# Fifteen small transfers on ScalarE's queue of a masked prefix-sum kernel

## The chip, the cores and the metric

The kernel runs on one core of a Trainium2 chip. The metric is the device time of one execution in microseconds; the time before is the median of 8 runs. A profile of one execution is read beside it: its span runs from the first instruction to the last.

## The reference

For each of 8 batches, x is masked beyond the batch's length, summed along the sequence, and the running sum at the middle of the length is taken; that row is multiplied by w.

```python
B, S, D = 8, 8192, 512                       # x [B,S,D], w [D,D], float32
mask = (pos < lengths[:, None, None])
cs = np.cumsum(x * mask, axis=1)
mid_features = cs[b_idx, lengths // 2, :]
return np.matmul(mid_features[:, None, :], w).squeeze(1)
```

Only one row of the running sum is used, so what has to be computed for each batch is the sum of the first lengths//2 + 1 rows that are below the length, and then a product of 8 rows with w. With the lengths drawn, most of the time goes to reading some 27 MB of x.

## The kernel before

**Tiling.** x is cut into units of 8 rows (8 x 512 floats, 16 KB). A chunk is 128 units, one for each partition: 2 MB. The first 256 rows of each batch come as two front chunks, by two plain transfers on SP's queue at the start. The units beyond are packed: VectorE computes from the lengths how many chunks there are and a table `idx` of unit numbers, and GpSimd fetches each chunk by an indirect DMA (11 of them here). A last part is fetched in two halves into `xl`, then 256 rows (from row 256 on) of two batches into `xb`, and w in three slices into `wt`.

**Ring.** Chunks land in four slots of `xt`. TensorE multiplies a chunk's units with 0/1 weights (`wr`, made by VectorE, copied into the slot by ScalarE) and adds into `s_ps`, 8 matmul calls a chunk (16 matmul records). When a chunk is done, GpSimd issues the gather that reuses its slot (`gather`, at L243 through `fetch`), and ScalarE copies the weights of the chunk that comes there (`weigh`, L206). SP's `relay` (L174) waits for the weights and for the landing and tells TensorE, which waits at L455. Between chunks TensorE runs idle matmuls (L446) into an unused bank.

**End.** The last part, `xb`, the folding of the partial sums (`mf_ps`), and the product with w (`o_ps`) follow. VectorE copies one half of the output and SP stores it; ScalarE copies the other half (L215) and stores it itself (L222). GpSimd waits for both stores.

**ScalarE's program** is what the change touches, in `scalar`. In its order: the transfer of the lengths (L516, issued ahead of the program's branch), the clearing of `xl` (L187, `s_zero`), a wait for VectorE's mark "w", a load of `count` (L191), the copy of the weights of the last part (L194, `wl`), the weights of chunks 2 and 3 (L198), the ring of `weigh`, the two copies of the output and the store. GpSimd waits for `s_zero` before it fetches into `xl`. Each engine issues its transfers on a queue of its own (SP q1, ScalarE q10, GpSimd q0); all are carried out by the same 16 DMA engines of the core. A transfer raises its semaphore by 16 when all of it has landed.

Of the kernel before, what the change touches and what calls it, by code (L numbers as in the profile page):

```python
# [11 lines left out]
P = 128  # L12
# [3 lines left out]
def kernel(  # L16
# [17 lines left out]
    B, S, D = x.shape  # L34
# [23 lines left out]
    def sb(name, shape, dt=F32):  # L58
        return ctx.enter_context(nc.sbuf_tensor(name, shape, dt))

    def ps(name, shape):
        return ctx.enter_context(nc.psum_tensor(name, shape, F32))

    def sem(name):
        return tc.alloc_semaphore(name)
# [52 lines left out]
    c_sb = sb("c_sb", [P, P])  # L118
    mf_sb = sb("mf_sb", [P, KC, B])
    o_sb = sb("o_sb", [P, D // 2])  # L120

    s_ps = ps("s_ps", [P, D])
    c_ps = ps("c_ps", [P, D])
# [7 lines left out]
    s_front = [sem(f"front{k}") for k in range(FRONT)]  # L131
    s_last = [sem(f"last{k}") for k in range(HALF)]
    s_back = [sem(f"back{k}") for k in range(BB)]
    s_w = [sem(f"w{k}") for k in range(3)]
    s_len, s_out, s_pool, s_dve, s_pe, s_done, s_wr, s_rdy, s_zero, s_act, s_wl, s_now = (
        sem(n) for n in ("len", "out", "pool", "dve", "pe", "done", "wr", "rdy", "zero", "act", "wl", "now"))
# [6 lines left out]
    def weights_of(s):  # L143
        return wr[:, s * U * B:(s + 1) * U * B]

    def ring(eng, name, left, body):
        for s in range(R):
            with nc.body(f"{name}_0_{s}", valid_engines=[eng.engine]):
                eng.br_cmp(left, s, f"{name}_1_{s}", f"{name}_end", "IS_GT")  # L149
            with nc.body(f"{name}_1_{s}", valid_engines=[eng.engine]):  # L150
                body(s)
                if s == R - 1:
                    eng.reg_sub(left, left, R)
                eng.br(f"{name}_0_{(s + 1) % R}")
# [30 lines left out]

    def scalar(act):
        act.memzero(xl[:]).then_inc(s_zero, 1)  # L187
        left = act.alloc_register("left_act")
        free = act.alloc_register("free_act")
        act.wait_ge(s_dve, marks["w"])  # L190
        act.load(left, count[:])  # L191
        act.reg_sub(left, left, 1)
        last = act.snap(left)
        act.copy(out=wl[:], in_=wc[:, bass.ds(last, 1)].rearrange("p c e -> p (c e)"),  # L194
                 ).then_inc(s_wl, 1)
        act.reg_add(left, left, FRONT)
        for s in range(FRONT, R):
            act.copy(out=weights_of(s), in_=wc[:, s - FRONT]).then_inc(s_wr, 1)  # L198
        act.reg_sub(left, left, R)
        act.reg_mov(free, 1)  # L200
        act.br("ac_0_0")

        def weigh(s):
            act.wait_ge(s_done, free)
            col = act.snap(free)
            act.copy(out=weights_of(s),  # L206
                     in_=wc[:, bass.ds(col + (R - FRONT - 1), 1)].rearrange("p c e -> p (c e)"),
                     ).then_inc(s_wr, 1)
            act.reg_add(free, free, 1)

        ring(act, "ac", left, weigh)
        with nc.body("ac_end", valid_engines=[act.engine]):
            act.wait_ge(s_pe, 6)
            for j in range(2):
                act.copy(out=o_sb[64:64 + B, j * P:(j + 1) * P],  # L215
                         in_=o_ps[64 + 32 * j:64 + 32 * j + B, :P]).then_inc(s_act, 1)
            act.wait_ge(s_act, 2)
            store(act, 1)
            act.br(END)

    def store(eng, g):
        eng.dma_start(out=out[:, HALVES[g]], in_=o_sb[64 * g:64 * g + B]).then_inc(s_out, 16)  # L222
# [201 lines left out]
    def tensor(pe):  # L424
# [81 lines left out]
        with nc.body("pe_pad", valid_engines=[pe.engine]):  # L506
            for _ in range(PAD):
                pe.wait_ge(s_dve, 1)
            pe.br("pe_0")

    programs = [(nc.vector, vector, "dv"), (nc.sync, sync, "sy"), (nc.scalar, scalar, "ac"),
                (nc.gpsimd, gpsimd, "gp")]
    for f in range(FRONT):
# [42 lines left out]
```

## Time and profile before

| what | us |
|---|---|
| median of 8 runs | 83.33 |
| lowest and highest of them | 82.88, 84.48 |
| the profiled execution | 82.9 |
| its span | 81.1 |
| TensorE busy, weight loads beside it | 56.6, 15.0 |
| VectorE, ScalarE, GpSimd busy | 14.1, 8.1, 20.5 |

The span has 1120 instructions, and the granted clock is 0.997. The transfers, from the profile's rows of DMA queues:

```profile
DMA packets 2789, 31.25 MB, mean 385 GB/s; under 512 B 370, under 2 KB 386, under 8 KB 898
q1 hardware_dynamic: 304, 4.20, 12.4%
q8 instruction: 1, 0.02, 0.1%
q14 instruction: 2, 0.02, 0.0%
```

Each row gives packets, megabytes and the time that the packets took as a share of 16 engines' span. In the timelines below a row is: start in us, length in us, engine, line, operation, output<-input, number, and in brackets the idle time ahead of it with what ended it. A row of stages gives the stage, its length, the busy time of PE, PEld, DVE, ACT and POOL with the number of instructions, the granted clock, the DMA share and the GB/s.

### The profile page before, as it was taken

To read this page: it belongs to the slowest core of one execution; us is meant where nothing else is said; L and a number is where in the kernel's file an instruction comes from. 1 tells how busy PE (TensorE), PEld (TensorE's weight loads), DVE (VectorE), ACT (ScalarE), POOL (GpSimd) and SP (SyncE) were. 2 spreads that over 40 slices of the span, in tenths; PEclk is the share of its full clock that TensorE was granted. 3 is DMA by queue.
4 is the path that set the end of the run, shared out by engine and by line. 5 is a ranking of instruction groups with operands and counts; after the bars stand their busy time and mean duration, and the time that the engine had idled before them with its cause. 6 is when DMAs were issued, how large, how long until landed. Compare 5 with 4: busy or idle time off the path is not lost. (4 is left out here: it accounts for less than half of the span.)

```text
span 81.1 us, 1120 instructions
## 1 busy us (share of the span) xinstructions
PE 56.6 (70%) x358; PEld 15.0 (19%) x358; DVE 14.1 (17%) x58; ACT 8.1 (10%) x16; POOL 20.5 (25%) x43
## 2 busy tenths in 40 slices
PE   1962399996939589393975939679394984848830
PEld 1462121212102021120201102021120201005600
DVE  4738899610000000000000000000000000004220
ACT  2991000310100001010010100100000000000020
POOL 4400644524050501405032050569600000000000
PEclk9999999999999999999999999999999999999998
DMA  0999999999999999999999999999999999999400
GB/s 0 364 412 388 493 404 396 461 412 408 420 445 428 420 437 433 420 437 429 437 428 428 420 445 420 429 437 428 420 437 437 412 408 412 404 412 408 178 0 8
DMA packets 2789, 31.25 MB, mean 385 GB/s; under 512 B 370, under 2 KB 386, under 8 KB 898
## 3 DMA queue, kind: packets, MB, share of 16 engines
q0 software_dynamic: 2464, 27.00, 78.9%
q1 hardware_dynamic: 304, 4.20, 12.4%
q8 instruction: 1, 0.02, 0.1%
q10 hardware_dynamic: 18, 0.01, 0.0%
q14 instruction: 2, 0.02, 0.0%
HBM read 31.46 MB, written 0.02 MB: 388 GB/s over the span
## 5 line engine op out<-in xcount | busy, mean ns | idle before, releaser
L426 PE MATMUL s_ps<-xt,wr 128*8 128x512 f32 x208 | 26.1, 621 | 15.1 <-PEq L455 15.1
L446 PE MATMUL idle_ps<-rank,v_f 128*4 128x512 f32 x48 | 22.6, 593 | 0.0
L426 PEld LDWEIGHTS s_ps<-xt,wr 128*8 128x8 f32 x208 | 5.0, 90 | 34.9 <-issue 34.9
L243 POOL DMA_INDIRECT xt<-in_x_dram,now x9 | 9.2, 1021 | 8.0 <-POOLq L269 8.0
L298 DVE COPY s_sb<-s_ps 128x256 f32<-128x256 f32 x2 | 0.8, 424 | 56.9 <-PE s_ps L426 56.8
L267 POOL COPY now<-idx 128x1 int32 x9 | 2.5, 279 | 22.1 <-PE s_ps L426 22.1
L446 PEld LDWEIGHTS idle_ps<-rank,v_f 128*4 128x4 f32 x48 | 4.2, 88 | 16.6 <-issue 16.6
L206 ACT COPY wr<-wc 128x64 f32 x9 | 2.2, 244 | 32.9 <-PE s_ps L426 32.7
L243 POOL DMA_INDIRECT xt<-in_x_dram,idx x2 | 2.2, 1119 | 5.8 <-DVE at_f L298 5.5
L187 ACT ACTIVATE xl<-xl 128x4096 uint32<-128x4096 uint32 x1 | 3.6, 3617 | 0.0
L434 PE MATMUL s_ps<-zero 1*128 1x512 f32 x2 | 2.1, 1136 | 1.8 <-DVE jump L298 1.8
L215 ACT COPY o_sb<-o_ps 8x128 f32<-8x128 f32 x2 | 0.5, 256 | 26.9 <-PE o_ps L426 26.9
L426 PE MATMUL s_ps<-xl,wl 128*8 128x512 f32 x16 | 2.1, 594 | 1.3 <-DMA xl<-in_x_dram,idx_h 1.3
L298 DVE TENSOR_TENSOR wc<-early,ge 128x1984 f32<-128x1984 f32 x1 | 2.2, 2225 | 0.0
L298 DVE TENSOR_TENSOR early<-v,b_ps 128x1984 f32<-128x1984 f32 x1 | 2.2, 2222 | 0.0
L438 PE MATMUL b_ps<-row,ones 1*128 1x16 f32 x2 | 0.6, 380 | 2.3 <-DVE row L298 2.3
L243 POOL DMA_INDIRECT xl<-in_x_dram,idx_h x2 | 2.0, 992 | 0.6 <-issue 0.6
L426 PE MATMUL c_ps<-xb,wb 128*2 128x128 f32 x32 | 1.3, 276 | 0.3 <-DMA xb<-in_x_dram 0.2
L187 ACT ACT_TABLE_LOAD x1 | 1.3, 1283 | 1.5 <-SPq L56 1.5
L426 PE MATMUL o_ps<-wt,mf_sb 128*8 128x128 f32 x32 | 1.2, 273 | 0.3 <-DVE mf_sb L298 0.3
L492 PE MATMUL mf_ps<-fold,s_sb 128*128 128x8 f32 x8 | 1.2, 264 | 0.0
L492 PEld LDWEIGHTS mf_ps<-fold,s_sb 128*128 128x128 f32 x8 | 1.1, 193 | 0.5 <-issue 0.5
(74 smaller groups left out, 22.9 us busy)
## 6 DMA issues: line engine op xcount, KB each, us to landing
xt<-in_x_dram SPq DMA_DIRECT2D x2, 2048.0 KB, 10.4
xb<-in_x_dram POOLq DMA_DIRECT2D x2, 512.0 KB, 18.4
wt<-in_w_dram POOLq DMA_DIRECT2D x1, 512.0 KB, 19.5
wt<-in_w_dram POOLq DMA_DIRECT2D x2, 256.0 KB, 19.6
xt<-in_x_dram,now POOLq DMA_INDIRECT x9, 16.0
xt<-in_x_dram,idx POOLq DMA_INDIRECT x2, 11.9
xl<-in_x_dram,idx_h POOLq DMA_INDIRECT x2, 17.3
lens<-in_lengths_dram ACTq DMA_DIRECT2D x1, 0.1 KB
```

The source lines that it names most:

```text
L187: act.memzero(xl[:]).then_inc(s_zero, 1)
L206: act.copy(out=weights_of(s), in_=wc[:, bass.ds(col + (R - FRONT - 1), 1)].rearrange("p c e -> p (c e)"),).then_inc(s_wr, 1)
L215: act.copy(out=o_sb[64:64 + B, j * P:(j + 1) * P], in_=o_ps[64 + 32 * j:64 + 32 * j + B, :P]).then_inc(s_act, 1)
L243: pool.indirect_dma_start(out=to, out_offset=None, in_=units, in_offset=bass.IndirectOffsetOnAxis(ap=at, axis=0), bounds_check=n - 1, oob_ ...
L267: pool.tensor_copy(out=now[:, s:s + 1], in_=idx[:, bass.ds(col + (R - FRONT - 1), 1)],).then_inc(s_now, 1)
L298: do(*args, **kw).then_inc(s_dve, 1)
L426: return pe.matmul(to[32 * j:32 * j + weights.shape[1], :rows.shape[1]], lhsT=weights, rhs=rows, start=False, stop=False, skip_group_check ...
L434: pe.matmul(to[:, :width], lhsT=zero[:, :P], rhs=zero[:, :width], start=True, stop=False, skip_group_check=True)
L438: pe.matmul(to[:, :of.shape[1]], lhsT=ones[:], rhs=of[:], start=True, stop=True,).then_inc(s_pe, 1)
L446: pe.matmul(idle_ps[:FB], lhsT=v_f[:, 0], rhs=rank[:].to_broadcast((P, D)), start=True, stop=True, skip_group_check=True)
L492: pe.matmul(mf_ps[:, B * k:B * (k + 1)], lhsT=s_sb[:, at], rhs=fold[:], start=False, stop=False, skip_group_check=True)
```

## The change

A tile `small` of 128 x 512 floats and a semaphore `s_small` are added. Behind the clearing of `xl` ScalarE issues fifteen transfers: the k-th takes the first k rows and k+16 columns of w into k rows of `small`, at a column of its own. Nothing reads `small`. Ahead of its store ScalarE waits until `s_small` has reached 240, that is, until all fifteen have landed. No other instruction is added, removed or moved on any engine.

```diff
     o_sb = sb("o_sb", [P, D // 2])
+    small = sb("small", [P, D])
...
     s_back = [sem(f"back{k}") for k in range(BB)]
+    s_small = sem("small")
...
     def scalar(act):
         act.memzero(xl[:]).then_inc(s_zero, 1)
+        for k in range(1, 16):
+            act.dma_start(out=small[:k, 32 * k:33 * k + 16], in_=w[:k, :k + 16]).then_inc(s_small, 16)
         left = act.alloc_register("left_act")
...
             act.wait_ge(s_act, 2)
+            act.wait_ge(s_small, 240)
             store(act, 1)
```

## The prediction

> **What bounds the kernel now.** I read the page's strip of slices first, then the stages by windows, then the chain that ended last, then ScalarE's own timeline, and at last the single packets and the landing records of the DMA rows.
>
> ```profile
> DMA  0999999999999999999999999999999999999400
> q0 software_dynamic: 2464, 27.00, 78.9%
> q10 hardware_dynamic: 18, 0.01, 0.0%
> L426 PE MATMUL s_ps<-xt,wr 128*8 128x512 f32 x208 | 26.1, 621 | 15.1 <-PEq L455 15.1
> ```
>
> The 16 DMA engines are 90% busy or more in 36 slices of 40; TensorE idles 15.1 us ahead of its chunk matmuls, at L455, where it waits for a chunk to land. ScalarE's queue is q10: 18 packets, nearly nothing.
>
> ```profile
> 13.00:19.00 6.00, 5.14 (x28) 0.99 (x30) 2.74 (x10) 1.02 (x5) 3.18 (x4) 1.00 1.03 434
> 19.00:35.00 16.00, 12.10 (x76) 2.52 (x76) 0.00 (x0) 0.73 (x3) 3.71 (x7) 1.00 1.00 427
> 35.00:55.00 20.00, 14.81 (x89) 2.97 (x82) 0.00 (x0) 0.98 (x4) 6.38 (x10) 1.00 1.01 430
> ```
>
> The last two numbers of each stage are the DMA share and GB/s: full, at 427 to 434. One chunk is 2 MB, 8 packets of 16 KB on each engine; the packets' rows say 611 ns each, and 8 x 0.611 = 4.89 us is the period of the chunks. So the end is set by DMA time, and by the DMA engine that finishes last.
>
> ```profile
> 55.98 18.73 DMA xb<-in_x_dram
> 74.71 0.04 issue
> 74.75 0.63 PE c_ps L426 x12
> ```
> ```profile
> 77.30 0.12 PEld L426 LDWEIGHTS o_ps<-wt,mf_sb 128*8 128x8 f32 x8 [0.24 <-DMA wt<-in_w_dram]
> ```
>
> The chain ends in the landing of xb, and its last matmuls wait for the last slice of w, which landed at 77.26. That landing is a record of 16 marks, one for each engine: twelve between 76.18 and 76.47, then 76.64, 76.90, 77.16 and 77.26. Four engines lag, and two of them (call them A and C) are 0.7 to 1.0 us behind the twelve. Each lag starts at a code packet: 16 KB on q8 at 2.22 (927 ns), and 8 KB on q14 at 19.34 and 30.88 (314 and 309 ns), after which the next data packet took 1107, 1136 and 881 ns. From then on the lags stay the same to the end. Twelve engines have 0.79 to 1.08 us to spare, the others 0.62, 0.36, 0.10 and 0: what is added on an engine with time to spare costs nothing, what is added on A or C moves the end one for one.
>
> ```profile
> 0.92 0.53 ACTq L516 DMA_DIRECT2D lens<-in_lengths_dram  x1
> 1.49 1.28 ACT L187 ACT_TABLE_LOAD   x1 [1.49 <-SPq L56]
> 2.79 3.62 ACT L187 ACTIVATE xl<-xl 128x4096 uint32<-128x4096 uint32 x1
> 15.29 0.25 ACT L194 COPY wl<-wc 128x64 f32 x1 [8.88 <-DVE wb L298]
> 78.34 0.56 ACTq L222 DMA_DIRECT2D out_dram<-o_sb  x1
> ```
>
> **Part 1: fifteen issues on ScalarE's sequencer.** A row costs 0.53 (lens, one packet) or 0.56 us (the store, eight); SP's two of 128 packets took 1.30 together. So 15 x 0.53 to 15 x 0.66 = 8.0 to 9.9 us. They stand behind the clearing of xl and before the wait for VectorE's w mark. In this trace ScalarE's register steps run before its copies are done (the step of L199 at 15.43, the second copy of L198 at 15.58), so I let the issues start near 2.8, beside the clearing, and end near 11 to 13; at the latest they start when it ends, at 6.41, and end at 14.4 to 16.3. The w mark lets ScalarE go at 14.38 before. At worst its copies come 1.9 us later. What is queued behind them is wl (used at 70.05) and the weights of chunk 2: the first of these is copied at 15.44, and that chunk lands at 18.79, so over 3 us cover it. Past that, TensorE would take chunk 2 late, and GpSimd's next gather would wait; but gathers land 16 us after their issue at one each 4.9 us, so some 11 us of transfers are queued. Cost 0; it costs something only if ScalarE is late by more than these 11 us. Nothing else is passed: lens is issued ahead of the fifteen, SP's front transfers and GpSimd's gathers are on other queues.
>
> A page speaks against such transfers: the Trainium skill, "DMA: Bandwidth & Descriptors", sections "Anatomy of one DMA — SWDGE (gpsimd) path" and "Rules for kernel authors", gives each a fixed 2.0 us, mostly overhead below 64 KB, so by it fifteen in a row would be an estimated 30 us. The row nearest is lens, 0.92 to its landing at 2.11, 1.19 us; fifteen of that in a row would be 18 us. Neither is on a path here, because nothing waits for one transfer before the next is issued, and the wait for all of them stands at 78 us.
>
> **Part 2: packets on the DMA engines.** Transfer k has k rows of (k+16) x 4 bytes, 68 to 124: 120 packets, 12.6 KB, in bytes 0.03 us of the 427 GB/s. What counts is the time per packet on one engine. The lens transfer of one row left one mark beside one packet, the store of 8 rows eight marks: each row goes to an engine of its own. So an engine gets at most 15 of the small packets and the mean over the engines is 7.5; which engine gets how many is not in the trace.
>
> The cost of one, from both sides. Low end: lens's packet of 64 bytes took 8 ns and a semaphore packet 9, and a gap of 4 ns stands between packets: 8 + 9 + 2 x 4 = 25 ns. A change of queue: at 12.4 to 12.7 the engines pass from q1 to q0, and the first 16 KB packet of q0 took 611 to 616 ns on ten of them and up to 820 on the others, 651 in the mean, 40 ns over; so 65 ns with that. High end: the store's 1 KB packets took 46 to 99 ns, and the packet after a code fetch lost 0.27 to 0.52 us. I take 25 to 65, since those small packets and that change of queue are of the same kind, with 45 in the middle. On A and C: 7.5 packets each in the mean, and the larger of two shares is near 10, so 10 x 0.045 = 0.45 us; the ends are 0 (A and C get none) and 15 x 0.065 = 0.98. The packets themselves can give no gain: the twelve engines at 611 ns run at their own pace and give nothing back to A and C.
>
> The same page, section "Why a DMA increments its semaphore by 16 and not by 1", says that k rows use the lowest-numbered k engines, which gives engine 0 fifteen and engine 14 one. It leaves open which numbers A and C have, so it changes the spread and not the mean.
>
> **Part 3: the last wait.** s_small reached 240 long before; the wait itself is one more instruction on ScalarE ahead of its store, 17 to 46 ns by other semaphore rows. The packets of SP's store start last (79.38 against 79.34), which covers it: 0 to 0.04, I take 0. The tile and the semaphore cost nothing.
>
> **The sum.** 0 + 0.45 + 0 on the profiled execution: span 81.1 to 81.5, time 82.9 to 83.35. That execution is 0.43 us below the median of 83.33 over 8 runs (82.88 to 84.48), so by the median 83.33 + 0.4 = 83.7.
>
> **The rivals.**
> 1. Hidden altogether: A and C get few small packets, or a packet costs its 17 ns alone. For it: twelve engines have 0.8 us or more to spare. Against it: C and A both have to be missed. Time 83.3.
> 2. Slower, each small packet breaks the stream of its engine. For it: the 0.27 to 0.52 us lost behind each code packet, which is also a lone packet of another queue. Against it: the change from q1 to q0 lost nothing on ten engines. At 0.1 us (the 1 KB rows) an engine with 15 of them is 1.5 us late, less up to 1.0 to spare: +0.5 to +1.5, about 84.4. At 0.27 it is 4.05 less 0.8: about 86.6. It decides from 0.09 us a packet on, where ten of them on A pass 1%.
> 3. One more code fetch: fifteen instructions more may push ScalarE's code over a block. One 8 KB packet with its loss is 0.31 + 0.27 to 0.31 + 0.52 on one engine, 0.6 to 0.8, which counts in full on A or C only: with part 2, up to 84.6.
> 4. Faster: the moved code lets a fetch fall on another engine. Without A and C's lag the end could come 0.4 us earlier, with all four gone 0.8, so that even this hardly reaches 1%: 82.5.
>
> **How the numbers follow.** My forecast (0.1 to 0.9 us, 83.4 to 84.2) 0.60; hidden 0.14; rival 2 0.17; rival 3 0.06; rival 4 0.03. A measurement here can tell about 1%, 0.8 us. Slower by more: rivals 2 and 3, and a little of my own upper end, 0.25; faster 0.03; within 1% 0.72. Range: from 83.0, just under the hidden case, to 84.9, which takes in the 0.1 us of rival 2 and rival 3, and leaves the broken stream out. The likeliest time is 83.7.
>
> **What would show it.** q10 should hold 258 packets (18 + 120 rows + 120 marks). ScalarE's queue should show fifteen issues of 0.53 to 0.66 us; a start before 6.4 shows that they pass the clearing, and wl should still come near 15.3. The chunk period should stay 4.89, and the waits of SP at L174 as they were. The 16 marks of the last landing decide part 2: if the last comes 0.1 to 0.9 us later and the middle of the twelve by less than that, the packets cost what I say. Packets of 16 KB of 700 ns and more beside the small ones, between 3 and 13 us, would show rival 2; a further packet on q8 or q14 rival 3. I am wrong if the stages from 19 to 55 us change their rate, since nothing of the change is left by then.

## The result, and the profile after

The changed kernel took 83.96 us in the median of 22 runs (83.55 to 84.93), the kernel before 83.28 us beside it (59 runs). The ratio is 1.0077, with a 95% interval of 1.0056 to 1.0099: 0.5 to 0.8 us slower, within the 1% that the forecast had as its likeliest case. Measured twice more, on two chips, the same change gave 1.0033 [1.0003, 1.0063] and 1.0029 [1.0005, 1.0054], some 0.25 us. The ratios leave out the single runs that a lower granted clock made slow, so they are not the quotients of the medians. Its profiled execution took 83.85 us, its span 82.0 us against 81.1.

First ScalarE's timeline of the changed kernel (start, length, engine, line, what):

```profile
0.92 0.53 ACTq L521 DMA_DIRECT2D lens<-in_lengths_dram  x1
1.48 1.28 ACT L189 ACT_TABLE_LOAD   x1 [1.48 <-SPq L56]
1.55 1.37 ACTq L191 DMA_DIRECT2D small<-in_w_dram  x4
2.78 3.62 ACT L189 ACTIVATE xl<-xl 128x4096 uint32<-128x4096 uint32 x1
2.94 4.25 ACTq L191 DMA_DIRECT2D small<-in_w_dram  x11
15.29 0.24 ACT L198 COPY wl<-wc 128x64 f32 x1 [8.89 <-DVE wb L303]
```

The fifteen issues begin before the clearing of `xl` has begun and run beside it; they take 5.6 us, 0.37 us each, and end at 7.2. The copy of `wl` stands at 15.29 as before. Then the page's rows of queues:

```profile
q10 hardware_dynamic: 258, 0.02, 0.2%
q8 instruction: 1, 0.02, 0.1%
q14 instruction: 2, 0.02, 0.0%
```

258 packets on ScalarE's queue, the 18 of before and 240 new ones (120 rows, 120 semaphore marks), and no further code packet. The chain still ends in the landing of `xb`, which comes 0.93 us later (75.64 against 74.71) at the same 18.73 us from issue to landing, and its last matmuls still wait for w:

```profile
56.92 18.73 DMA xb<-in_x_dram
75.64 0.04 issue
75.69 0.64 PE c_ps L431 x14
```
```profile
78.21 0.12 PEld L431 LDWEIGHTS o_ps<-wt,mf_sb 128*8 128x8 f32 x8 [0.21 <-DMA wt<-in_w_dram]
```

So the loss is made before 56 us and carried to the end. SP's waits for the landings say that it is made at the first gathers: for the two gathers with `idx` it waits 0.9 us longer, for the nine behind them as long as before (total, times, longest). Before, then with the change:

```profile
SPq L174 <- DMA xt<-in_x_dram,now: 42.0, 9, 4.7
SPq L174 <- DMA xt<-in_x_dram,idx: 8.9, 2, 4.7
```
```profile
SPq L176 <- DMA xt<-in_x_dram,now: 42.0, 9, 4.7
SPq L176 <- DMA xt<-in_x_dram,idx: 9.8, 2, 5.6
```

The stages show the place. A row gives the stage, its length, busy time of PE, PEld, DVE, ACT and POOL, the granted clock, the DMA share and the GB/s. Before:

```profile
9.00:12.40 3.40, 2.86 (x16) 0.61 (x17) 3.26 (x6) 0.00 (x0) 1.78 (x2) 1.00 0.96 410
12.40:13.60 1.20, 1.20 (x7) 0.26 (x3) 1.20 (x1) 0.00 (x0) 0.28 (x1) 1.00 0.96 396
13.60:18.00 4.40, 4.23 (x23) 0.73 (x20) 2.14 (x10) 1.02 (x5) 1.99 (x3) 1.00 1.02 428
```

With the change:

```profile
9.00:12.40 3.40, 2.86 (x16) 0.60 (x17) 3.26 (x6) 0.00 (x0) 1.78 (x2) 1.00 0.99 406
12.40:13.60 1.20, 1.20 (x5) 0.13 (x1) 1.20 (x1) 0.00 (x0) 0.00 (x0) 1.00 0.81 318
13.60:18.00 4.40, 4.40 (x22) 0.97 (x21) 2.14 (x10) 0.78 (x4) 1.74 (x2) 1.00 1.04 440
```

The middle rows differ. At 12.4 to 13.6 us the engines pass from the front transfers (q1) to the gathers (q0), which is called the hand-over below; there the DMA share is 0.81 where it was 0.96, and the rate 318 GB/s where it was 396. From 19 us on the stages run at 425 to 434 GB/s, as before.

The landing records say who is late. Each line holds marks of the last slice of w, one an engine, in us:

```
before   first 76.19, middle 76.38, last five 76.47 76.64 76.90 77.16 77.26
change   first 76.69, middle 76.83, last five 77.21 77.24 77.34 77.51 78.17
```

The middle moved by 0.45 us and the last by 0.91. The last engine is the one that took the 8 KB code packet at 19.07 us (309 ns, and 1146 for the data packet behind it): the last mark of the gather ahead of it stood 0.52 us behind the middle, that of the next 1.43. Before, one engine jumped the same way (code packet at 19.34 us; its mark is among those up to 17.98 us in one gather and at 23.67 or 23.71 in the next), but from at most 0.2 us behind the middle. So half of the 0.91 us is the middle's, and the rest comes mostly from which engine the code packet met. What is left after the last landing is unchanged, 2.60 us to the last mark of the stores (2.63 before).

### The profile page after: what moved, and what is told of

Same layout as the page of the kernel before. It is cut to its first block, busy times and chain, and to the rows that moved or that the text cites. A ratio compares the mean times of both kernels' runs of the same rounds, so it can differ in the third digit from the quotient of the medians.

```text
span 82.0 us, 1136 instructions
## 1 busy us (share of the span) xinstructions
PE 59.2 (72%) x358; PEld 15.9 (19%) x358; DVE 14.1 (17%) x58; ACT 8.1 (10%) x16; POOL 20.2 (25%) x43
## 3 DMA queue, kind: packets, MB, share of 16 engines
q1 hardware_dynamic: 304, 4.20, 12.4%
## 5 line engine op out<-in xcount | busy, mean ns | idle before, releaser
L431 PE MATMUL s_ps<-xt,wr 128*8 128x512 f32 x208 | 29.0, 655 | 13.4 <-PEq L460 13.4
L451 PE MATMUL idle_ps<-rank,v_f 128*4 128x512 f32 x48 | 24.4, 632 | 0.0
L431 PEld LDWEIGHTS s_ps<-xt,wr 128*8 128x8 f32 x208 | 5.7, 91 | 32.6 <-issue 31.8
L439 PE MATMUL s_ps<-zero 1*128 1x512 f32 x2 | 2.1, 1136 | 1.8 <-DVE jump L303 1.8
```

What stands on the lines that cost most here:

```text
L431: return pe.matmul(to[32 * j:32 * j + weights.shape[1], :rows.shape[1]], lhsT=weights, rhs=rows, start=False, stop=False, skip_group_check ...
L439: pe.matmul(to[:, :width], lhsT=zero[:, :P], rhs=zero[:, :width], start=True, stop=False, skip_group_check=True)
L451: pe.matmul(idle_ps[:FB], lhsT=v_f[:, 0], rhs=rank[:].to_broadcast((P, D)), start=True, stop=True, skip_group_check=True)
```

## The experiments

Each kernel was measured beside the kernel before on the same chip; all but the repeats are edits of the changed kernel. Two numbers are read from the records of every profile, and stand in the table behind the experiments: the time at which the mean engine lands a gather, and the time that the 16 engines together stand without a packet between 12.4 and 13.6 us.

**Every transfer twice.**

```diff
         for k in range(1, 16):
-            act.dma_start(out=small[:k, 32 * k:33 * k + 16], in_=w[:k, :k + 16]).then_inc(s_small, 16)
+            for at in (32 * k, 32 * k + D):
+                act.dma_start(out=small[:k, at:at + k + 16], in_=w[:k, :k + 16]).then_inc(s_small, 16)
...
-            act.wait_ge(s_small, 240)
+            act.wait_ge(s_small, 480)
```

> The fifteen transfers, each issued twice: 240 small rows. Theory (each small transfer holds its DMA engine for some 60 ns, and the end moves with the engine that finishes last, which carries nearly all fifteen): the middle of the 16 landing marks of the last slice of w moved by 0.44 us with one set (76.38 to 76.82) and should move by 0.9 with two; the last mark moved by 0.91 (77.26 to 78.17) and should move by 1.5 to 1.8; ratio to before 1.014 to 1.020. Rival A (a cost paid once, by the hand-over from the front transfers to the gathers or by a code packet that falls on another engine): marks and ratio as with one set, 1.008. Rival B (ScalarE's issues are late and hold up the weights): the copy of wl moves from 15.29 and the ratio grows with it.

84.84 us against 83.38, ratio 1.0132 [1.0077, 1.0187]. The ratio's interval still touches that of the change, but the marks moved as the theory asked: the middle one of the last slice of w by 1.08 us against the first profile (to 77.46), the last by 1.72 (to 78.98). So the cost grows with the rows and isn't paid once, and `wl` is copied at 15.29 again: rival A falls, and so does rival B. But a third code packet appeared (27.16 us), which the page's rows count:

```profile
q10 hardware_dynamic: 498, 0.03, 0.5%
q8 instruction: 1, 0.02, 0.1%
q14 instruction: 3, 0.02, 0.1%
```

so the kernel is not the change doubled and nothing more.

**Fifteen transfers of one row; eight of fifteen rows.**

```diff
+            act.dma_start(out=small[:1, 32 * k:33 * k + 16], in_=w[:1, :k + 16]).then_inc(s_small, 16)
```
```diff
+        for k in range(8):
+            act.dma_start(out=small[:15, 32 * k:32 * k + 24], in_=w[:15, :24]).then_inc(s_small, 16)
```

> Fifteen transfers as before in number, but each of one row: 15 small rows in all. Theory (time on an engine; a one-row transfer uses one engine, the same each time): the middle of the landing marks stays where it was before (76.4), one mark moves by some 0.9 us. If that engine is the one that came last with the change, the last mark is near 78.1 and the ratio near 1.008; if it is another, the last mark is near 77.3 and the ratio at most 1.002. Rival A (the small rows slow all engines together, through the memory): an eighth of the effect, ratio 1.001, and no mark stands out. Rival B (the fifteen issues, not the rows): ratio 1.008 with the middle mark moved as with the change.

> Eight transfers of fifteen rows: 120 small rows as with the change, but spread evenly, eight on each of fifteen engines. Theory (time on an engine): fifteen marks move by 8 x 60 ns = 0.5 us, one stays; the last mark moves by 0.5 where the change moved it by 0.91; ratio 1.005 to 1.006. Rival A (all engines slowed together by the number of rows): the same as the change, 1.008. Rival B (the number of issues): half of the change, 1.004, whatever the marks.

One row each: 83.44 against 83.38, ratio 1.0000 [0.9971, 1.0029]. So fifteen issues on ScalarE cost nothing that can be told from zero (0.3% at most), and neither do fifteen rows on one engine that has time to spare. At 47 us four marks are late where the late kernel measured beside it (next experiment, which has no small rows by then) shows three, and the last is where it is there: 48.70 and 48.65. Fifteen rows each: 83.87, ratio 1.0046 [1.0012, 1.0080]. This interval holds the theory's 1.005, the 1.004 of rival B (which the one-row kernel rules out) and the repeats of the change, so the time settles nothing here; but the mean engine moved by some 0.3 us (table) and not by 0.5, so the price of a row was too high.

**The same transfers late.** The loop is moved behind ScalarE's ring, ahead of the wait for the output.

> The same fifteen transfers, issued after ScalarE's last copy of weights (some 51 us) and not at 1.5 us, when all code packets have passed. Theory (time on an engine counts the same wherever it falls, while the engines are full): up to 50 us the marks are those of before, at the end the middle has moved by 0.45 and the last by up to 0.9; ratio 1.005 to 1.008. Rival A (a cost of the first 20 us, the hand-over from the front transfers to the gathers or the code packet at 19 us): ratio 1.000 to 1.002.

83.74 against 83.38, ratio 1.0028 [0.9994, 1.0062]: near a third of the first measurement, and not to be told from nothing. The marks up to 50 us are those of a kernel without small rows, and at the end the middle stands at 76.74, where 47.56 at the gather of 47 us and the 29.12 us of before make 76.68: it moved by 0.06 and not by 0.45. The mean of the sixteen moved by 0.14, as 120 rows of 19 ns make it. (In this profile the granted clock fell in the last slices, and the last 32 matmuls took 1.77 us where 1.20 is usual, so its span says nothing.) By the marks it matters where the rows fall, which the theory denied; the time doesn't show it, since the repeats of the change below stand at the same ratio.

**The kernels before and after once more.**

> The kernel before, once more, for its landing marks beside those of the other kernels of this call. If marks belong to the engines and the program, the last slice of w lands as in the first profile: mean of the 16 marks near 76.5, twelve within 0.4 us, the last 0.9 to 1.1 behind the middle. If the 0.3 us between the profiles of one call (e3 and e5 before 50 us against the first profile) is the spread of executions, this one falls between 76.4 and 76.9.

> The changed kernel, once more. Theory (time on an engine): the mean of the 16 marks is 0.3 to 0.5 us later than that of before in this call (120 rows x 40 to 60 ns / 16), the last mark 0.5 to 0.9 later; ratio 1.006 to 1.010. If a row costs only its own 21 ns, the mean is 0.16 later and the last mark at most 0.3.

Before: mean 76.84, last mark 77.44, so executions differ by 0.2 to 0.4 us in all marks together. The last mark of the first front transfer, too, stands 0.70 to 1.80 us behind the middle in the four profiles that have no small row by then (both of before, the late one, and the one behind the weights below), so that the engine it belongs to is sometimes the one that ends last, rows or not. After: ratio 1.0033 [1.0003, 1.0063]; mean 77.21, last mark 78.19, 0.37 and 0.75 over before measured beside it. A price of 21 ns alone makes 0.16 and at most 0.3; but with such a spread of executions one profile of each doesn't settle it.

**The price of a row, measured by itself.**

```diff
+        for k in range(40):
+            act.dma_start(out=small[:8, 24 * k:24 * k + 24], in_=w[:8, :24]).then_inc(s_small, 16)
```

> Forty transfers of eight rows of 96 bytes, at the same place: forty rows on each of eight engines, none on the other eight. Theory (a row costs its engine some 60 ns): the 16 marks of the last slice split into eight as before and eight that are 2.4 us later, and the end moves by 1.4 to 2.4 us, ratio 1.017 to 1.029. If a row costs 21 ns, its own two packets, the eight are 0.84 us later and the end moves by 0.8 or less, ratio at most 1.010. Rival A (all engines slowed together): the marks do not split. Which of the late marks (those behind a code packet) lie among the eight shows to which half their engines belong.

> The same forty transfers with rows of 512 bytes and not 96. At the rate of the 16 KB packets (611 ns) 416 bytes more are 16 ns more a row, so the eight marks are 0.6 us later than with 96 bytes if only the bytes count. If a row under 512 bytes pays extra for being small, the eight marks come no later or earlier than with 96 bytes.

Marks of the last slice of w, in us:

```
96 B    76.49 76.56 76.57 76.59 76.61 76.66 76.70 | 77.33 77.56 77.60 77.61 77.62 77.80 78.18 78.30 79.11
512 B   76.53 76.56 76.61 76.64 76.71 76.72 76.93 | 78.15 78.18 78.26 78.34 78.53 78.69 79.44 79.85 80.66
```

The marks split. Seven engines are where they were; the body of the others stands 1.0 us later (77.6 against 76.6), so a row of 96 bytes costs 1.0 / 40 = 25 ns: its packet (12 ns in the records), its semaphore packet (9) and the gap. A row of 512 bytes stands 1.65 us later, 41 ns, and its packet took 27 ns. So the 416 bytes more cost 16 ns, as they do in the 16 KB packets, and a row under 512 bytes pays nothing extra for being small. The times, ratio 1.0203 [1.0155, 1.0251] and 1.0350 [1.0291, 1.0408], are above that; ScalarE's forty issues also brought a third code packet (23.6 and 23.2 us), which is the likely reason. That the first ratio lies in the range of the 60 ns is luck: the marks rule that price out. The engine that ends last carries rows: from its mark at 30.21 us to that at 50.16 it fell back by 0.33 us more against the seven (2.37 to 2.70), as some 13 rows of 25 ns make it, and no code packet is that small.

**The wait moved to GpSimd; long rows on four engines.**

```diff
-            act.wait_ge(s_small, 240)
...
+            pool.wait_ge(s_small, 240)
             pool.drain()
```
```diff
+        for k in range(15):
+            act.dma_start(out=small[:4, D * k:D * k + D], in_=w[:4]).then_inc(s_small, 16)
```

> The changed kernel with the wait for s_small moved from ScalarE's store to GpSimd, which waits for the stores anyway. Theory (the wait is hidden): nothing changes, ratio as the change, 1.003 to 1.008, and 2.6 us between the last mark of w and the last mark of the stores, as before. Rival (the wait on ScalarE holds up the store): back by up to 0.1 us, ratio lower by 0.001.

> Fifteen transfers of four rows of 2 KB: fifteen rows on each of four engines, each row 76 ns + 9 + 4 by the forty-row kernels, 1.34 us an engine. Four marks of the last slice stand 1.3 us over where they would be. If one of the engines that take an 8 KB code packet is among the four, its mark is 1.3 over its old lag of 0.6 to 0.9: last mark near 78.9, ratio 1.016 to 1.020. If none is, the last mark is near 78.2, ratio 1.007 to 1.011, and the jump of 0.8 at the code packets is seen on marks that are not among the four.

The wait: 84.03 against 83.28, ratio 1.0089 [1.0047, 1.0130], and 2.61 us from the last mark of w to the last of the stores. It is hidden.

The long rows fell out of every expectation: 86.76 us, ratio 1.0408 [1.0361, 1.0454]. Eleven marks stand at 76.30 to 76.68, four at 77.50 to 78.65, and one at 80.91. On that one engine the 16 KB packets beside the long rows took 844, 847, 852 and 1048 ns between 14.9 and 19 us, where those of the other engines took mostly 611. This is the second rival of the prediction, on one engine of 16, with rows of 2 KB. Why that engine alone isn't known, and no later run repeats it.

**Behind the hand-over.** The loop is moved behind ScalarE's copies of the weights of chunks 2 and 3; the changed kernel runs beside it.

> The fifteen transfers of the change, issued behind ScalarE's copies of the weights of chunks 2 and 3 (15.6 us), when the front transfers are over and the gathers run. Theory now (a row costs its own packets, 25 ns, up to 0.375 us on an engine; the rest of the change's cost is the hand-over from the front transfers to the gathers at 12.4 to 13.6 us, where the 16 engines together stand idle 2.9 to 4.9 us with the change and 0 to 0.1 without): no idle at the hand-over, mean of the marks 0.2 to 0.3 us over before, ratio 1.001 to 1.004. Rival (a row costs 45 to 60 ns wherever it is): idle or not, mean 0.35 to 0.45 over before, ratio 1.005 to 1.008, as the change in the same call.

> The changed kernel on the chip of this call, as the partner of the kernel behind the weights. Ratio 1.004 to 1.009 from the two measurements so far (1.0077 and 1.0033); idle of the 16 engines between 12.4 and 13.6 us 2.5 to 5 us in all. If the hand-over is what counts, it lies 0.2 to 0.4 us above its partner; if the rows alone count, the two are equal.

83.55 and 83.68 us against 83.48: ratios 1.0020 [0.9997, 1.0043] and 1.0029 [1.0005, 1.0054]. The two lie 0.1 us apart and not the 0.2 to 0.4 that were expected if the hand-over counts; the intervals overlap, so the times don't settle it. The stages do show what was expected, here the kernel with the transfers behind the weights:

```profile
9.00:12.40 3.40, 2.21 (x12) 0.48 (x16) 3.26 (x6) 0.00 (x0) 1.78 (x2) 1.00 1.01 434
12.40:13.60 1.20, 1.20 (x9) 0.18 (x2) 1.20 (x1) 0.00 (x0) 0.00 (x0) 1.00 1.03 410
```

and its partner, the change for the third time:

```profile
9.00:12.40 3.40, 2.86 (x16) 0.61 (x17) 3.26 (x6) 0.00 (x0) 1.78 (x2) 1.00 1.07 454
12.40:13.60 1.20, 1.20 (x5) 0.13 (x1) 1.20 (x1) 0.00 (x0) 0.00 (x0) 1.00 0.85 320
```

The table has both numbers for all kernels but the doubled and the long ones. The mean is counted from the first data packet of the 16 engines to their marks of the gather that lands at 47 us.

| kernel | DMA share 12.4 to 13.6 us | engines idle there, us in all | mean to the gather's marks, us |
|---|---|---|---|
| before, twice | 0.96, 1.00 | 0.02, 0.00 | 44.80, 44.92 |
| the transfers at 51 us (no row yet) | 1.00 | 0.12 | 45.01 |
| fifteen of one row | 1.01 | 0.00 | 45.04 |
| behind the weights | 1.03 | 0.00 | 45.23 |
| eight of fifteen rows | 0.74 | 1.26 | 45.28 |
| the change, three times | 0.81, 0.80, 0.85 | 2.93, 4.92, 1.92 | 45.25, 45.54, 45.40 |
| the wait moved | 0.62 | 4.06 | 45.51 |
| forty of eight rows | 1.05 | 0.29 | 45.68 |

The sum, for the mean engine: without rows 44.91; with the change (four profiles) 45.42, so 0.51 more. 120 rows at 25 ns are 3.0 us, 0.19 an engine; the idle time at the hand-over, 3.46 us in the mean, is 0.22 an engine; 0.10 is left, within the 0.2 by which the profiles without rows differ. Behind the weights 0.32 more: 0.19, no idle, 0.13 left.

Most of that spread is there when the first front transfer lands. Counted from the mean of its marks instead, the three profiles without rows agree to 0.04 (39.35 to 39.39 us), the kernel behind the weights stands 0.07 over their mean, and the change 0.20 to 0.54 over it (four profiles). So on the mean engine the place of the rows, ahead of the hand-over, costs more than the rows themselves. What is shown is the time of the mean engine; how much of it the last engine passes on to the kernel's time isn't.

The doubled kernel, which the table leaves out, loses more than such a sum gives: its mean is 46.01, 1.10 over, where 240 rows at 25 ns are 0.38. Its engines are behind for longer, at 293 GB/s from 12.4 to 13.6 us and still 377 from 13.6 to 18, where the kernel before has 428. With forty rows of 512 bytes the mean is 46.30, 1.39 over, with no idle at the hand-over; the rows at 41 ns are 0.82, and the rest stays open.

## Why the prediction was right, point by point

**ScalarE.** Cost 0 was right. The issues took 0.37 us each, not 0.53 to 0.66, and passed the clearing: the kernel with fifteen one-row transfers is at 1.0000. The fixed 2.0 us a transfer that the Trainium skill gives ("DMA: Bandwidth & Descriptors", "Anatomy of one DMA — SWDGE (gpsimd) path") was fitted there to transfers that GpSimd issues, which these aren't. On the slowest engine the fifteen did land one behind the other, at 1.2 us each; but nothing waited for them, as argued.

**Packets on the engines.** The mechanism was right: time on an engine counts only where that engine ends last, 258 packets came, and the last landing moved by 0.91 us, just past the 0.1 to 0.9 that was asked of it. Two steps in it were off, in opposite directions, so that the sum of 0.45 us came out near the measured ones (0.64, 0.28 and 0.24 us) in part by luck.
- The price of a row, 25 to 65 ns with 45 in the middle: 25 by the forty-row kernel. The 40 ns for a change of queue were wrong. They were read at the hand-over from q1 to q0 of the profile before, and are not paid by each row.
- What was missing is the hand-over with rows in front of it, 2 to 5 us over the engines. Most engines run out of the front transfers and of the small rows, and the gathers' first packets start 0.1 to 0.3 us an engine after that: on q0 the first begins at 12.77 to 12.88 us in the four profiles of the change, and at 12.37 to 12.64 in those without rows there. That the idle time belongs to rows queued there is shown by moving them: it is gone in both kernels that issue them later, and small (0.29 us) with forty rows an engine, perhaps because such a stock lasts until the gathers come. Why the gathers' first packets come later was not tried.

**"A and C get 7.5 rows in the mean, the larger share near 10."** The engine that ends last carries rows (forty-row kernel), and it is hardly the single engine of the one-row kernel: fifteen rows of 25 ns are 0.375 us, 1.0045, above that kernel's interval. In the profile of the change it isn't the engine with all fifteen either: that one's turns go on every 0.61 us from 18.6 to 21.67 us, while the late engine spent 19.07 to 20.53 on its code packet and the packet behind it. How many rows the late one has stays open. That eight rows go to eight engines and no others is what the split of the marks shows, seven apart from the rest (one late engine without rows stands among the others); the rule that these are the lowest-numbered ones ("Why a DMA increments its semaphore by 16 and not by 1") no run here can show.

**The rivals.** Hidden altogether: ruled out, no interval of the change (nor that of the moved wait) reaches 1. Each row breaks the stream: at 0.1 us and more a row, ruled out by 25 ns a row; it happened on one engine with rows of 2 KB. But the sign that was named for it, 16 KB packets of 700 ns and more beside the rows, is there in part: between 6 and 12.3 us 8 to 12 such packets in three profiles of the change and none in the fourth, and none in the four profiles without rows by then. All that the packets there took over 611 ns is 1.6 to 2.9 us over the 16 engines, 0.10 to 0.18 an engine, as much as the sum above leaves or more. What such packets lose on the engines with rows is within the 25 ns, which counts all that these engines lost against the others. One more code fetch: not with fifteen transfers, but with thirty and with forty, each time as a third packet on q14. Faster: nothing of it.

**The last wait.** 0, as 2.60 and 2.61 us show. (The 79.38 and 79.34 us by which SP's packets were said to start last are the ends of the last packets; they start in the same order, at 79.33 and 79.26.)

## What to carry to other kernels

In a kernel that fills its DMA engines, a side transfer costs what its packets take on the engine that ends last, so look at the marks of the last landing, one an engine, before calling a transfer free or dear. Here fifteen rows on one engine cost nothing that could be told from zero, and 120 rows in a ladder over fifteen engines cost 0.2 to 0.8 us. Look also at the point where one queue runs out and another takes over, since small rows queued there left the engines idle, and count the instructions that the transfers add: code is fetched by the same engines.

## What the runs showed of the hardware

- A small transfer's row and its semaphore mark each wait their turn behind a 16 KB packet: on the slowest engine the fifteen rows and fifteen marks of the change lasted from 3.94 to 21.68 us, 29 turns of 0.61 us. In time on the engine they cost 25 ns a row; in latency 1.2 us each.
- An 8 KB code packet costs its engine 0.6 to 0.9 us: 0.31 itself, and the rest in the data packet behind it (near 19 us 1136 to 1231 ns before and with the change, near 31 us 881 to 961, against 611). Two such packets, with the 16 KB one at 2.2 us, make most of the late engines in this kernel.
- In some executions the granted clock fell for some slices. Where that was the end, the last 32 matmuls took 1.77 and 1.90 us and not 1.20.
